# Preparing group A's first job inside the projection's stage

## The chip, the cores and the metric

The kernel runs on one core of a Trainium2 chip, in one launch. The metric is the device time of a run in microseconds, smaller is better. A core has five engines with a queue of instructions each, which they work off strictly in the order in which the program was laid out: TensorE (PE; its weight loads are listed as PEld), VectorE (DVE), ScalarE (ACT), GpSimd (POOL) and SyncE (SP, which here issues most of the transfers between HBM and SBUF). They wait for each other only through semaphores.

## The reference, cut to what matters

Two layers, 1024 tokens, width 1024. In each layer one input projection makes the columns of four head groups A to D, each group mixes the tokens in its own way, an output projection joins them, and a hierarchical mixture of experts follows. Everything is float32.

```python
h = rms_norm(x, norm1_g[l]) * (1 + sc1) + sh1
p = h @ w_in[l]                                  # 1024 x 3244
pA, pB, pC, pD = split_cols(p, (A_COLS, B_COLS, C_COLS, D_COLS))
yA = rwkv7_time_mix(pA, ...)       # A: state recurrence over the tokens
yB = stick_breaking_attn(...)      # B
yC = mlstm_mix(pC, ...)            # C: short convolution, then mLSTM
yD = dsa_attn(...)                 # D: top-256 keys per query, then attention
x = x + gt1 * (jnp.concatenate([yA, yB, yC, yD], -1) @ w_out[l])
x = x + gt2 * hier_moe(rms_norm(x, norm2_g[l]) * (1 + sc2) + sh2, ...)
```

The part of group A that this case is about is elementwise work on r, k, v, the decay and the in-context rate, before the recurrence runs:

```python
p = token_shift(p, mu)
r, k, v, wd, ad, gd = split_cols(p, A_SIZES)
kk = (k * k_k).reshape(B, S, H, d)
kk = kk / jnp.maximum(jnp.sqrt(jnp.sum(kk * kk, -1, keepdims=True)), 1e-12)
k = k * (1 + (a - 1) * k_a)
bonus = jnp.sum(r_h * k_h * r_k.reshape(H, d), -1, keepdims=True) * v_h
```

## The kernel before

**Stages of a layer.** First the hidden state is made and split into a high and a low float32r part, together with the indexer's columns of group D. Then comes the projection's stage, then the mixing stage with all four groups and the output projection, then routing and the experts. The two layers have the same stages; in layer 0 the mixing stage also computes the adaLN rows of later use (transfers and products named `aw`).

**The projection's stage.** `proj_rest` (L1933) goes through a list of jobs, one block of columns of `w_in` each. For each block it fetches the weights two blocks ahead (`fetch`, tiles `wr`), splits them one block ahead into `wh` (ScalarE) and `wl` (VectorE for the later blocks, L1863), and then runs the products. A block of 128 transposed columns is done in two halves of 512 tokens (`proj_t`, L1867), 24 products each into one PSUM tile `pj`, of which there are three. Seven blocks of group A come near the end, in the order 6, 0, 2, 4, 1, 3, 5 (here A6, A0, ...): A6 holds the low-rank inputs, A0 and A1 are r, A2 and A3 are k, A4 and A5 are v. The last four blocks are group C's, here C0 to C3. `take` (L255) empties a half of an A block: ScalarE makes `u`, VectorE makes `p` (L265), and SyncE stores `p` to HBM. `take_t` does so for C, with three VectorE operations L679, one L682 and a sigmoid (`cs`).

Beside it runs `select`, the search for each query's top 256 keys: rounds of counting on VectorE (L1022) and ScalarE (`eq`), each followed by small steps (L1087, L1089, L1084), and a tail (L1104 to L1111).

**Group A's jobs.** The recurrence is cut into four jobs (two column tiles ct by two halves hf of the tokens). `prep` (L287) prepares one: six transfers bring back what `take` and `lowrank` stored (L296 to L301), then a chain goes through all engines: a square on ScalarE, a product `pn` with a 0/1 matrix on TensorE, VectorE L307, ScalarE's Ln and Exp, VectorE L311, a scan L315, L314, L319 to L322, exponentials on ScalarE, L338 and the GpSimd operations L313 and L339 that make `ar`, L341, L342, L345, L346, a second product from `bon`, and L350. Each job then has four units; a unit starts with four transposes (L148, from `ar`, `kn`, `ks`, `v`) and small products into `pj`. `Rwkv.run` (L503) prepares the first job, then keeps three units going and prepares the later jobs beside them.

**What sets the order.** `weave` (L196) asks generators for their next piece of work, by a virtual clock that advances with the TensorE work that each has issued, and a generator that yields `WAIT` is asked again later. That gives the program order. From it the framework's scheduler lays out each engine's queue, with the program order as priority, and a tile can only be written once a buffer of its pool is free: 23 buffers in `big`, 38 in `med`. The queues are fixed before the kernel runs. Before the change, the first job was emitted by the first steps of `rw.run()`, in the second `weave`:

```python
weave(k, [(proj(), 257)], [(select(), 100)])
weave(k, [(rw.run(), 260)], [(dsr(), 350), (rest(), 140)], [(mods(), 550)], [(outs(), 150)])
```

`dsr` is group D's attention; its blocks for eight tiles of queries start with products into `a`, a masked maximum on VectorE (L1128, `dz`), an exponential on ScalarE, and transposes of `dz`.

Of the kernel before, what the change touches and what calls it, by code (L numbers as in the profile page):

```python
# [30 lines left out]
A0, B0, C0, D0 = 0, 896, 1664, 2696  # L31
# [63 lines left out]
class K:  # L95


    def __init__(self, ctx, tc, nbig, nmed, consts_dram):
        self.tc, self.nc, self.n = tc, tc.nc, 0
        self.ctx = ctx  # L100
        self.bigp = ctx.enter_context(tc.tile_pool(name="big", bufs=nbig))
        self.medp = ctx.enter_context(tc.tile_pool(name="med", bufs=nmed))
        self.cp = ctx.enter_context(tc.tile_pool(name="cp", bufs=1))
        self.sp = ctx.enter_context(tc.tile_pool(name="sp", bufs=2))
        self.ps = ctx.enter_context(tc.tile_pool(name="ps", bufs=1, space=PSUM))
        self.cst = self.cp.tile([P, NCONST], F32, name="cst")
        self.nc.sync.dma_start(self.cst, consts_dram[:, 0:NCONST])
        t = self.med("lev", 384)
        self.nc.sync.dma_start(t, consts_dram[:, NCONST:NCONST + 384])
        self.lev = self.cp.tile([P, 384], BF16, name="levb")  # L110
        self.nc.vector.tensor_copy(self.lev, t)
        self.evn, self.pe = 0, 0.0
        self.mode, self.mode_load, self.mode_acts = None, None, []
# [79 lines left out]
WAIT = -1.0  # L193


def weave(k, *streams):  # L196

    live = [[0.0, list(s)] for s in streams]
    while live:
        s = min(live, key=lambda x: x[0])
        gen, pace, *prio = s[1][0]
        before = k.pe
        try:
            if prio and prio[0]:
                with k.tc.high_priority(offset=prio[0]):
                    other = next(gen)  # L210
            else:
                other = next(gen)
        except StopIteration:
            s[1].pop(0)
            if not s[1]:
                live.remove(s)
            continue
        if other == WAIT and len(live) > 1:
            s[0] = 0.002 + min(x[0] for x in live if x is not s)
        else:  # L220
            s[0] += (k.pe - before + (other or 0.2)) / pace
# [23 lines left out]
class Rwkv:  # L245


    def __init__(self, k, pc, lw, rst, tk, l):
        self.k, self.pc, self.lw, self.rst = k, pc, lw, rst
        self.tk, self.l = tk, l  # L250
        self.s, self.y, self.done = {}, {}, set()

# [246 lines left out]
        yield  # L501

    def run(self, width=3):  # L503
        self.job = {}
        jobs = [(ct, hf) for hf in range(2) for ct in range(2)]
        yield from self.prep(*jobs[0])
        units = [(ct, 0, nb) for ct in range(2) for nb in range(4)] + [(ct, 1, nb) for nb in range(4) for ct in range(2)]
        ahead = {(0, 0, 1): jobs[1], (1, 0, 0): jobs[2], (1, 0, 2): jobs[3]}
        live, side = [], []
        k = self.k  # L510
        free = [(k.med("ra"), k.med("bkv", 384), k.med("mp"), k.med("tl")) for _ in range(width)]
        while units or live or side:
            while units and len(live) < width and units[0][:2] in self.job and "bon" in self.job[units[0][:2]]:
                u = units.pop(0)
                own = free.pop(0)
                live.append((u, self.unit(*u, own), own))
                if u in ahead:
                    side.append(self.prep(*ahead[u]))
            for it in list(live):
                try:  # L520
                    next(it[1])
                    yield
                except StopIteration:
                    live.remove(it)
                    free.append(it[2])
                    if it[0][2] % 2:
                        side.append(self.out(*it[0][:2], it[0][2] // 2))
            for g in list(side):
                try:
                    next(g)  # L530
                    yield
                except StopIteration:
                    side.remove(g)
# [1093 lines left out]
class Trunk:  # L1627
# [337 lines left out]
    def layer(self, l):  # L1965
        k, nc, ins = self.k, self.nc, self.ins
        pc = self.pc(l)
        ml = Mlstm(k, pc, self.gb, self.idb, self.mneg4.rearrange("p h t -> p (h t)"), self, l)
# [4 lines left out]
        rw = Rwkv(k, pc, self.lw, self.rst, self, l)  # L1973
        rw.eps = self.eps[:, 1:2]

        def take_b(j, h, ps):
# [4 lines left out]
            for x, st in enumerate((hi, lo)):  # L1981
                self.store_t(l, "b", 4 * x + j, h, st.bitcast(F32))

        bind = lambda f, j: lambda h, ps: f(j, h, ps)
        by_t = lambda c0, f, js: [(c0 + 128 * j, 128, lambda w, j=j: self.proj_t(w, bind(f, j))) for j in js]
        by_k = lambda c0, col, f: [(c0, 256, lambda w: self.proj_k(l, w, col, f))]
        bq = by_t(B0, take_b, range(4))
        jobs = (bq[:1] + by_k(B0 + 512, 0, AF.Copy) + [(D0 - 8, 264, lambda w: self.proj_q(ds, ml, w))]
                + bq[1:2] + by_k(C0 + 512, 256, AF.Copy) + bq[2:3]
                + [(C0 + 768, 256, lambda w: gate_out(w))] + bq[3:]  # L1990
                + by_t(A0, rw.take, (6, 0, 2, 4, 1, 3, 5)) + by_t(C0, ml.take_t, range(4)))

        def gate_out(w):
            ml.tanh()
            yield from self.proj_k(l, w, 512, AF.Sigmoid)

        def select():
            yield from ds.scores()
            yield from ds.search()

        sb = Stick(k, pc)
        sb.eps = self.eps[:, 0:1]
        stage = set()
        until = lambda f: iter(lambda: None if f() else WAIT, None)

        def proj():
            yield from self.proj_rest(l, jobs)
            stage.add("proj")
# [6 lines left out]
        def rest():  # L2015
            yield from until(lambda: "proj" in stage)
            ys[6], ys[7] = (both(ds.y, c) for c in range(2))
            ml.load(self, l)
            yield from ml.run()
            ys[4], ys[5] = (both(ml.y, c) for c in range(2))  # L2020
            yield from sb.run(self, l)

        def dsr():
            yield from until(lambda: "proj" in stage)
            yield from ds.run()
# [46 lines left out]
        def mods():  # L2072
            yield from until(lambda: "proj" in stage)
            if l == 0:
                yield from self.ada(0, [1])
            gt1.append(self.mod(l, 2))
            if l == 0:
                yield from self.ada(0, [2])
                yield from self.ada(1, [0, 1, 2])

        weave(k, [(proj(), 257)], [(select(), 100)])
        weave(k, [(rw.run(), 260)], [(dsr(), 350), (rest(), 140)], [(mods(), 550)], [(outs(), 150)])
        drain([moe.route()])
        gt2 = self.mod(l, 5)
# [128 lines left out]
```

## Time and profile before

| | us |
|---|---|
| median of three runs | 3555.73 |
| lowest and highest of them | 3541.35, 3557.87 |
| the profiled execution, its own time | 3548.04 |
| its span on the core | 3546.3 |
| TensorE busy | 3119.6 (88%) |
| VectorE busy | 2668.3 (75%) |
| ScalarE busy | 1953.8 (55%) |

How to read it: the profile is of one execution. Busy shares are averages over stages with different limits, so the stage around the change is read by itself: from windows (busy time of each engine, granted TensorE clock as a share of 2.4 GHz) and from the timeline (start, length, engine, line, operation, and in brackets the idle time before and who ended it). Matmuls overlap, so their rate is the distance between starts. In layer 0 the projection's stage lies before 433 us and the mixing stage behind it, in layer 1 the border is near 2191 us.

### The profile page before, as it was taken

What the parts mean: (1) busy time and instruction counts of PE and PEld (TensorE: products, weight loads), DVE (VectorE), ACT (ScalarE), POOL (GpSimd) and SP (SyncE); (2) the same over time, 40 slices, a digit from 0 to 9 for tenths busy, and PEclk for the clock granted to TensorE, in tenths of its full rate; (3) what the DMA queues carried; (4) which work ended last, traced back from release to release, by engine and by line L of the source; (5) the groups of instructions that cost most, each with busy time, mean ns of one, the idle gap of its engine ahead of it and who ended that gap; (6) DMA issues with size and microseconds to landing.
All of it is one profiled execution on the core that took longest, in us unless ns stands there. A gap on an engine that the chain in (4) does not pass through costs nothing. (4 is left out here: it accounts for less than half of the span.)

```text
span 3546.3 us, 58612 instructions
## 1 busy us (share of the span) xinstructions
PE 3119.6 (88%) x20960; PEld 2412.4 (68%) x20960; DVE 2668.3 (75%) x5190; ACT 1953.8 (55%) x3452; POOL 817.9 (23%) x769
## 2 busy tenths in 40 slices
PE   5988889989878899999968898988987889999996
PEld 3876645576656677777758766766665667877775
DVE  3589853467666899999975898556666689999995
ACT  3469333234443667777753782533444366777774
POOL 3220110113221225432212201011321221332231
PEclk8999989899887899999989998989988789999998
DMA  5233365443525799999942333124352479999996
GB/s 200 72 96 99 103 221 202 164 148 102 152 91 185 267 375 385 376 386 381 388 131 63 99 99 102 32 69 148 102 149 93 179 271 365 386 382 381 381 387 209
DMA packets 373685, 746.67 MB, mean 211 GB/s; under 512 B 44234, under 2 KB 108512, under 8 KB 373392
## 3 DMA queue, kind: packets, MB, share of 16 engines
q1 hardware_dynamic: 346880, 671.84, 52.5%
q0 software_dynamic: 20256, 70.33, 7.6%
q8 instruction: 167, 2.74, 0.3%
q10 hardware_dynamic: 6256, 0.74, 0.1%
q14 instruction: 126, 1.03, 0.1%
HBM read 635.26 MB, written 107.53 MB: 209 GB/s over the span
## 5 line engine op out<-in xcount | busy, mean ns | idle before, releaser
L160 ACT ACTIVATE wh<-wr 128x1024 fp32r<-128x1024 f32 (+3 forms) x900 | 887.9, 1006 | 297.1 <-DMA wr<-in_moe_w_dram 118.8
L1530 DVE TENSOR_TENSOR wl<-wr,wh 128x1024 fp32r<-128x1024 f32 x792 | 941.9, 1225 | 58.1 <-ACT wh L160 45.9
L143 PE MATMUL pj<-wl,xh 128*128 128x512 f32 x1056 | 419.5, 404 | 14.1 <-DVE wl L1530 13.7
L143 PE MATMUL pj<-wh,xh 128*128 128x512 f32 x1056 | 421.3, 400 | 11.7 <-ACT xh L160 10.3
L143 PE MATMUL pj<-wh,xl 128*128 128x512 f32 x1056 | 420.0, 398 | 0.0
L143 PEld LDWEIGHTS pj<-wl,xh 128*128 128x128 f32 x1056 | 200.4, 190 | 82.1 <-DVE wl L1530 37.8
L143 PEld LDWEIGHTS pj<-wh,xh 128*128 128x128 f32 x1056 | 199.9, 190 | 56.7 <-ACT xh L160 12.9
L143 PEld LDWEIGHTS pj<-wh,xl 128*128 128x128 f32 x1056 | 201.0, 190 | 45.5 <-DVE xl L1542 0.8
L143 PE MATMUL b<-wh,hh 128*128 128x512 f32 x528 | 210.9, 400 | 11.0 <-ACT wh L160 10.0
L1426 POOL DMA_INDIRECT xg<-h2d,si x64 | 76.3, 1193 | 606.1 <-PE a L148 349.7
L143 PE MATMUL b<-wh,hl 128*128 128x512 f32 x528 | 208.6, 395 | 1.1 <-DVE hl L1542 1.1
L143 PE MATMUL pj<-hh,wh 128*128 128x512 f32 x480 | 195.4, 409 | 8.8 <-ACT wh L160 8.4
L143 PE MATMUL pj<-hh,wl 128*128 128x512 f32 x480 | 195.9, 409 | 2.2 <-DVE wl L1863 2.2
L143 PE MATMUL pj<-hl,wh 128*128 128x512 f32 x480 | 194.2, 405 | 0.0
L1497 POOL DMA_INDIRECT xs<-yo,si x32 | 162.5, 5078 | 135.7 <-DVE yo L1494 111.1
L143 PE MATMUL pj<-wh,hl 128*128 128x256 f32 (+2 forms) x640 | 188.0, 296 | 1.8 <-DVE hl L1840 1.7
L143 PE MATMUL pj<-wh,hh 128*128 128x256 f32 (+2 forms) x640 | 182.0, 296 | 5.2 <-ACT wh L160 2.4
L143 PE MATMUL pj<-wl,hh 128*128 128x256 f32 (+2 forms) x640 | 184.2, 290 | 1.1 <-POOL wl L1863 1.1
L143 PE MATMUL b<-wl,hh 128*128 128x512 f32 x528 | 175.6, 412 | 6.9 <-DVE wl L1530 6.8
L1497 POOL DMA_INDIRECT out_dram<-yo,si x32 | 141.7, 4429 | 132.9 <-DVE yo L1494 116.7
L160 ACT ACTIVATE ra<-b 128x128 f32<-128x128 f32 (+1 forms) x192 | 54.1, 293 | 160.0 <-PE b L143 158.4
L143 PEld LDWEIGHTS pj<-wh,hh 128*128 128x128 f32 x640 | 121.5, 195 | 9.2 <-ACT hh L160 3.5
(526 smaller groups left out, 7374.0 us busy)
## 6 DMA issues: line engine op xcount, KB each, us to landing
wr<-in_moe_w_dram SPq DMA_DIRECT2D x792, 512.0 KB
aw<-in_ada_w_dram SPq DMA_DIRECT2D x96, 512.0 KB
wr<-in_w_in_dram SPq DMA_DIRECT2D x84, 256.0 KB
wo<-in_w_out_dram SPq DMA_DIRECT2D x48, 256.0 KB
xs<-xp SPq DMA_DIRECT2D x48, 256.0 KB
xp<-xs SPq DMA_DIRECT2D x48, 256.0 KB
out_dram<-xp SPq DMA_DIRECT2D x48, 256.0 KB
sk<-pt SPq DMA_DIRECT2D x32, 256.0 KB
```

Source lines behind the costliest of these rows:

```text
L143: return self.nc.tensor.matmul(out, lhsT, rhs, start=start, stop=stop, skip_group_check=True)
L160: i = self.nc.scalar.activation(out, in_, f, **kw)
L1426: i = self.k.nc.gpsimd.indirect_dma_start(out=xg, out_offset=None, in_=self.h2d, in_offset=bass.IndirectOffsetOnAxis(ap=gi.bitcast(U32), a ...
L1497: k.nc.gpsimd.indirect_dma_start(out=self.xs, out_offset=bass.IndirectOffsetOnAxis(ap=si.bitcast(U32), axis=0), in_=yo, in_offset=None, co ...
L1530: i = nc.vector.tensor_tensor(wl, raw, wh.bitcast(F32), op=ALU.subtract)
```

## The change

Group A's first job, ct 0 and hf 0, is now prepared by a third generator of the first `weave`, `first_job`. It waits until the second half of block A4 has been taken; with A6, A0 and A2 done before, all rows of that job exist then. `Rwkv.run` skips the preparation if it is there. Nothing is computed differently and no line inside `prep` changes.

```diff
-        self.s, self.y, self.done = {}, {}, set()
+        self.s, self.y, self.done, self.job = {}, {}, set(), {}
...
     def run(self, width=3):
-        self.job = {}
         jobs = [(ct, hf) for hf in range(2) for ct in range(2)]
-        yield from self.prep(*jobs[0])
+        if jobs[0] not in self.job:
+            yield from self.prep(*jobs[0])
...
+        def take_a(j, h, ps):
+            rw.take(j, h, ps)
+            stage.add(("a", j, h))
+
+        def first_job():
+            yield from until(lambda: ("a", 4, 1) in stage)
+            yield from rw.prep(0, 0)
...
-                + by_t(A0, rw.take, (6, 0, 2, 4, 1, 3, 5)) + by_t(C0, ml.take_t, range(4)))
+                + by_t(A0, take_a, (6, 0, 2, 4, 1, 3, 5)) + by_t(C0, ml.take_t, range(4)))
...
-        weave(k, [(proj(), 257)], [(select(), 100)])
+        weave(k, [(proj(), 257)], [(select(), 100)], [(first_job(), 100)])
```

**VectorE behind block A4, layer 0.** `p_3427` is the second half of A4; `wr_3347` and `wr_3349` are the raw weights of A3, and the `wl` made of them are its low parts. Before:

```order
L265 SCALAR_TENSOR_TENSOR p_3427<-pj_3401,drv,u_3426 128x512
L1087 TENSOR_TENSOR dth_2212<-dth_2212 128x3
L1089 SCALAR_TENSOR_TENSOR dth_2212<-dth_2212 128x3
L1084 TENSOR_SCALAR dth_2212<-dth_2212 128x3
L1863 TENSOR_TENSOR wl_3449<-wr_3347,wh_3448 128x512
L1022 TENSOR_SCALAR dkey_2215,dth_2212<-dkey_2215,dth_2212 128x768
```

Now the same split stands 45 rows behind `p_3427`; these are the last of them, with the job's own rows L322, L345, L350 and L346 and the search's between:

```order
L345 SCALAR_TENSOR_TENSOR bon_3488<-la_3433,prm,ks_3452 128x512
L1022 TENSOR_SCALAR dkey_2215,dth_2212<-dkey_2214,dth_2212 128x640
L1089 SCALAR_TENSOR_TENSOR dth_2212<-dth_2212 128x3
L322 TENSOR_TENSOR f_3465<-f_3465 128x7
L1022 TENSOR_SCALAR dkey_2216,dth_2212<-dkey_2214,dth_2212 128x384
L1084 TENSOR_SCALAR dth_2212<-dth_2212 128x3
L1087 TENSOR_TENSOR dth_2212<-dth_2212 128x3
L1022 TENSOR_SCALAR dkey_2215,dth_2212<-dkey_2215,dth_2212 128x768
L1089 SCALAR_TENSOR_TENSOR dth_2212<-dth_2212 128x3
L1863 TENSOR_TENSOR wl_3503<-wr_3347,wh_3502 128x512
L350 TENSOR_TENSOR bon_3488<-b_3491,v_3435 128x512
```

What moved: between `p_3427` and A3's first split lie now twelve counts L1022 of the search, with their small steps, and nine rows of the job (L307, L311, L315, L314, L319, L320, L321, L345, L322). On ScalarE, `wh_3502` stands in the same way behind the job's exponential of `cs`. In layer 1 it is ten counts and the same nine rows.

**TensorE at the end of the projection, layer 0.** The first row is the last product of block C3; `sq`, `bon`, `ar`, `kn`, `ks`, `v` are the job's tiles, `dz` and `dat` group D's. Before:

```order
L143 MATMUL pj_4106<-hl_348,wh_3957 128x512
L143 MATMUL pj_4238<-aw_4239,cz 32x512 x2
L143 MATMUL pj_4238<-aw_4241,cz 32x512 x2
L148 MATMUL pj_4257<-cst,dz_4226 128x128
L148 MATMUL pj_4261<-cst,dz_4247 128x128
L143 MATMUL b_4211<-sq_4209,cst 128x512
L143 MATMUL b_4264<-dat_4256,dv_325 64x128
L143 MATMUL b_4264<-dat_4260,dv_325 64x128
L143 MATMUL b_4304<-bon_4301,cst 128x512
L143 MATMUL a_4377<-dkh_439,dq_4222 128x384
```

Now:

```order
L143 MATMUL pj_4161<-hl_348,wh_4012 128x512
L148 MATMUL pj_4266<-cst,ar_3476 128x128
L148 MATMUL pj_4266<-cst,kn_3451 128x128
L148 MATMUL pj_4266<-cst,ks_3452 128x128
L148 MATMUL pj_4266<-cst,v_3435 128x128
L143 MATMUL pj_4273<-ar_3476,kn_3451 64x128 x2
L143 MATMUL pj_4273<-ar_3476,ks_3452 64x128 x2
L143 MATMUL pj_4279<-ar_3476,kn_3451 64x128 x2
L143 MATMUL pj_4279<-ar_3476,ks_3452 64x128 x2
L143 MATMUL pj_4302<-aw_4303,cz 32x512 x2
L143 MATMUL pj_4302<-aw_4305,cz 32x512 x2
L148 MATMUL pj_4321<-cst,dz_4289 128x128
```

What moved: the job's two products with the 0/1 matrix are gone from here (the first now stands inside the second half of A1, the second between A1 and A3), and the first unit's transposes and products stand right behind the projection, ahead of group D's transposes.

## Rows read from the trace of the kernel before

**Rows 1.** Windows: busy us (and count) by engine, granted clock, DMA share, GB/s.
```profile
330.00:400.00 70.00, 70.00 (x302) 56.73 (x301) 67.75 (x181) 40.66 (x78) 6.64 (x13) 1.00 0.30 93
433.00:458.00 25.00, 12.50 (x37) 4.04 (x35) 15.79 (x35) 9.43 (x24) 4.21 (x7) 0.59 0.55 186
443.90:450.50 6.60, 0.74 (x5) 0.35 (x5) 5.17 (x10) 2.77 (x6) 0.52 (x1) 0.50 0.98 362
460.00:1100.00 640.00, 566.23 (x5632) 381.94 (x5631) 370.50 (x858) 241.85 (x602) 118.05 (x189) 0.89 0.46 154
2191.00:2214.00 23.00, 9.08 (x23) 4.04 (x22) 14.90 (x33) 9.43 (x24) 4.04 (x6) 0.57 0.27 91
```

**Rows 2.** Timeline of TensorE, layer 0, from the projection's last product into the mixing stage.
```profile
433.00 0.40 PE L143 MATMUL pj<-hl,wh 128*128 128x512 f32 x1
...
440.68 0.86 PE L148 MATMUL pj<-cst,dz 128*128 128x128 f32 x2 [6.29 <-ACT dz L160]
...
450.35 2.07 PE L143 MATMUL b<-bon,cst 128*128 128x512 f32 x2 [5.86 <-DVE bon L345]
...
455.96 1.09 PE L148 MATMUL pj<-cst,dz 128*128 128x128 f32 x4
...
463.63 0.33 PE L148 MATMUL pj<-cst,ar 128*128 128x128 f32 x1
...
469.85 0.33 PE L148 MATMUL pj<-cst,ar 128*128 128x128 f32 x1
```

**Rows 3.** The same of layer 1.
```profile
2190.96 0.40 PE L143 MATMUL pj<-hl,wh 128*128 128x512 f32 x1
...
2212.56 1.18 PE L148 MATMUL pj<-cst,dz 128*128 128x128 f32 x4 [0.60 <-ACT dz L160]
...
2221.43 0.35 PE L148 MATMUL pj<-cst,ar 128*128 128x128 f32 x1
...
2225.33 0.27 PE L148 MATMUL pj<-cst,ar 128*128 128x128 f32 x1
```

**Rows 4.** Timeline of ScalarE, end of the projection: table load and two exponentials' groups.
```profile
438.84 1.28 ACT L154 ACT_TABLE_LOAD   x1
...
454.12 0.51 ACT L160 ACTIVATE dz<-dz,dnb 128x256 f32<-128x256 f32 x1 [3.29 <-DVE dnb L1132]
```

**Rows 5.** Timeline of VectorE: A4's second half in both layers, two search rounds.
```profile
351.94 0.75 DVE L265 SCALAR_TENSOR_TENSOR p<-pj,drv,u 128x512 f32<-128x512 f32 x1
...
359.75 0.88 DVE L1022 TENSOR_SCALAR_CACHE_REDUCE dkey<-dkey,dth 128x640 bf16<-128x640 uint16 x1
...
363.22 0.88 DVE L1022 TENSOR_SCALAR_CACHE_REDUCE dkey<-dkey,dth 128x640 bf16<-128x640 uint16 x1
...
2110.16 0.75 DVE L265 SCALAR_TENSOR_TENSOR p<-pj,drv,u 128x512 f32<-128x512 f32 x1
```

**Rows 6.** Timeline of ScalarE: A3's second half, taken as TensorE ends it, both layers.
```profile
371.98 0.69 ACT L160 ACTIVATE u<-pj,prm 128x512 f32<-128x512 f32 x1 [3.35 <-PE pj L143]
...
2130.11 0.69 ACT L160 ACTIVATE u<-pj,prm 128x512 f32<-128x512 f32 x1 [3.25 <-PE pj L143]
```

**Rows 7.** Timeline of TensorE behind its pause before block A0, layer 0.
```profile
323.09 0.79 PE L143 MATMUL pj<-hh,wh 128*128 128x512 f32 x1 [3.03 <-ACT wh L160]
...
325.25 0.63 PE L143 MATMUL pj<-hl,wh 128*128 128x512 f32 x1
...
330.37 0.50 PE L143 MATMUL pj<-hl,wh 128*128 128x512 f32 x1
330.71 0.39 PE L143 MATMUL pj<-hh,wh 128*128 128x512 f32 x1
```

**Rows 8.** Timeline of TensorE between blocks C1 and C2, layer 0.
```profile
404.90 0.40 PE L143 MATMUL pj<-hl,wh 128*128 128x512 f32 x1
...
408.30 0.49 PE L143 MATMUL pj<-hh,wh 128*128 128x512 f32 x1 [0.85 <-ACT wh L160]
...
409.70 0.63 PE L143 MATMUL pj<-hl,wh 128*128 128x512 f32 x1
```

More of the change, by code (lines that the diff above doesn't have):

```diff
@@ L1984, in layer @@
         bind = lambda f, j: lambda h, ps: f(j, h, ps)
+        stage = set()
+        until = lambda f: iter(lambda: None if f() else WAIT, None)
+        def take_a(j, h, ps):
[4 more added lines that the diff above has]
+            yield from rw.prep(0, 0)
         by_t = lambda c0, f, js: [(c0 + 128 * j, 128, lambda w, j=j: self.proj_t(w, bind(f, j))) for j in js]
@@ L2002, in layer @@
         sb.eps = self.eps[:, 0:1]
-        stage = set()
-        until = lambda f: iter(lambda: None if f() else WAIT, None)
         def proj():
```

## The prediction

> **What bounds the kernel now.** I read the windows first, then the timeline on both sides of the border between the projection and the mixing stage. In the projection's last part TensorE is the limit with VectorE right beside it: from 330 to 400 us TensorE is busy 70.0 of 70 us at the full clock (302 products, so one every 0.232 us, and a half block of 24 takes 5.56 us), and VectorE 67.8 of 70 [rows 1]. At the border TensorE starves: of the 25 us from 433 it is busy 12.5 at a granted clock of 0.59, of the 23 us from 2191 only 9.1 at 0.57 [rows 1]. The reader is to see two waits in it: 6.3 us for group D's first exponential, and 5.9 us for the job's `bon` on VectorE [rows 2]. After that TensorE is busy 566 of 640 us [rows 1], so the mixing stage is near its limit, but not at it.
>
> **The change, part by part.**
>
> *What leaves the border.* The first job's chain goes. In layer 0 the projection's last product starts at 433.00, so TensorE is free at E = 433.2; group D's second pair of transposes starts at 455.96, the transposes of the second and third unit at 463.63 and 469.85 [rows 2]. In layer 1: E = 2191.2, then 2212.56, 2221.43 and 2225.33 [rows 3].
>
> What is late next is group D's exponential. It comes behind group C's last sigmoid and a table load of 1.28 us [rows 4], and its transposes start 440.68 - 433.2 = 7.5 us after E [rows 2]. None of that moves, and two evacuations of the first unit now go ahead of it (0.6 us, an estimate by the exponential of 128 x 256 in [rows 4], which is of like size): 8.1. The next pair follows one masked maximum and two exponentials of 0.51 us later [rows 4], an estimate of 2 us: its transposes start at E + 10.1 instead of E + 22.8. From there the queue has the same pieces as before with a unit one further on, so before's way from 455.96 to 463.63, 7.7 us [rows 2], leads to the third unit: E + 17.8. In layer 1 that way is 8.9 us [rows 3], so E + 19.0.
>
> *What enters the projection: VectorE.* E does not stay where it is. The job is emitted right behind A4, before A3's weights are split, so it stands ahead of them in the order, and the title's "beside group C" is not where most of it lies. A3's `wl` now comes behind twelve counts of the search and nine rows of the job. Twelve counts are four double rounds of 363.22 - 359.75 = 3.47 us [rows 5], 13.7 without the last small step. The nine rows: VectorE was busy 5.17 us between 443.9 and 450.5, in ten instructions, one of them a copy of group D (0.3, estimated from what the nine leave): 4.9 [rows 1]. A4's `p` starts at 351.94 and takes 0.7 [rows 5], so A3's first low part is there at 352.6 + 13.7 + 4.9 + 0.6 = 371.8. When does TensorE want it? The second half of A3 ended at 371.9 before [rows 6], so A3 began 48 x 0.232 = 11.1 us earlier, at 360.8; one product of the job now lies ahead, 2.07 us at the low clock [rows 2], so 1.0 at the full one: 361.8. Wait: 10.0 us. The second product of the job lies within it.
>
> Layer 1: ten counts (11.7 us), so 2110.16 + 0.7 + 11.7 + 4.9 + 0.6 = 2128.1 [rows 5]; A3 would be wanted at 2130.1 - 11.1 + 1.0 = 2120.0 [rows 6]. Wait: 8.1 us.
>
> *The clock behind that wait.* After pauses of such a kind in layer 0 the products came every (330.37 - 325.25) / 12 = 0.427 us, the 1.2 GHz level, from 323.09 until 330.71 [rows 7], about 17 of them: 17 x 0.195 = 3.3 us. I take this for each layer. Bounds: nothing, if the clock holds, and twice as much.
>
> *The later waits.* Between C1 and C2 TensorE paused from 405.1 to 408.3 and came back at the low level (0.63 us a product) [rows 8]: 3.2 us and some 2 for the clock. C2's weights are split behind the search's tail and C0's evacuation. The job's six other rows and its nine put that tail some 9 us later, TensorE is about 10 later, so this pause shrinks: I give back 4 us. Bounds: 5 back, or 5 more.
>
> So E moves by 10.0 + 1.0 + 3.3 - 4 = 10.3 us in layer 0 and 8.1 + 1.0 + 3.3 - 4 = 8.4 in layer 1.
>
> *The other queues.* ScalarE gets the job's seven operations and one table load more per layer; it was busy 40.7 of 70 us [rows 1], and A3's `wh` comes before its `wl`, so VectorE ends the wait. On SyncE the job's first four transfers stand ahead of A3's raw weights, but these are asked for nearly two blocks ahead, over 20 us, so that hides them; without that cover A3 would wait for them instead. GpSimd's part ends long before a unit needs it. Nine `med` buffers are held through the projection: the order already contains that, as A1's evacuations now stand behind A3's split.
>
> *Sum.* Layer 0: group D's second pair at 433.2 + 10.3 + 10.1 = 453.6 instead of 455.96, 2.4 us sooner; the third unit at 461.3 instead of 469.85, 8.5 sooner. Layer 1: 2209.7 for 2212.56, 2.9 sooner; 2218.6 for 2225.33, 6.7 sooner. If the rest is bound by group A's chain of units, the gain is 15.2 us, if by the other streams and TensorE's work, 5.3. With 88% busy neither has it alone, so I take 10 us. The rest of the program has the same work, in an order that differs by a few dozen rows here and there.
>
> The profiled execution took 3548.0, so 3538; the median of the three runs is 7.7 higher, so 3546. I start from halfway, 3552, and say 3542 us.
>
> **Rivals.**
>
> *The whole gain (3523).* A3's weights are not late, since A1 to A5 have slack that I do not see. Then E stays and 18.7 us come on top: 24 to 34 us, in the middle 29. For it: TensorE loses its pause at the border. Against it: VectorE has 2.2 us free in 70 [rows 1] and gets 10 more per layer. The Trainium skill ("Perfetto Trace Analysis", Optimization Strategy) says that regimes with different most-contended engines may gain by being interleaved. By that rule this rival is the outcome. The trace agrees only by half, as the stage that takes the job in has its VectorE full too.
>
> *Nothing (3552).* The mixing stage is bound by TensorE's sum of work and idle time. The border loses 12.5 us of idle time and part of a low clock, and gets 10 and 8 us of idle time and a low clock in the projection in return. For it: 88% busy [rows 1]. Against it: units wait for each other in a chain, and that chain starts earlier.
>
> *Slower (3567).* The wait spreads: with VectorE full, each later split (A5, C0, C2) also comes some 4 us late, so that E moves by 10 + 12 = 22. The start of the mixing stage is then late for both streams. It decides from where the gain is used up: for group D at 455.96 - 10.1 - 433.2 = 12.7 us in layer 0 and 11.3 in layer 1, for the units at 18.9 and 15.1. At 22 and 20 that is 3 to 9 us per stream and layer, 13 to 15 in sum, and beyond 25 it is over 20. For it: the tail of the search (L1104 to L1111) is VectorE's densest part. Against it: once the search is over VectorE has room. The Trainium skill ("Perfetto Trace Analysis", Optimization Strategy) has a rule that speaks this way too: bubbles that repeat on the engine which should be saturated can mean that buffers ran out for the next tile. No row of before shows it, as TensorE is busy throughout 330 to 400.
>
> **How the numbers follow.** The forecast gets 0.5, the whole gain 0.15, nothing 0.2, slower 0.15. The forecast's own range is 3530 to 3555. 0.5%, about what a measurement of this kernel can tell from no change, is 17.8 us. Faster by more: the whole gain and a fifth of the forecast, 0.25. Slower by more: two thirds of the slower case, and a little of the two middle ones, for a reordered schedule: 0.12. The rest, 0.63, is within. The range runs from 3518, below the whole gain, to 3570, which leaves out the upper end of the slower case.
>
> **What would show it.** Right: a pause of TensorE of 8 to 10 us between A1 and A3, ended by VectorE's `wl` (L1863), with 0.43 us products behind it; the projection's end 8 to 10 us later, relative to its start; at the border no wait for `bon`, the first unit's transposes at once, then a wait of some 6 us for `dz`; the third unit's transposes 18 to 19 us after E. Wrong: no pause before A3 (the whole gain), further pauses before A5, C0 or C2 (slower), or the third unit earlier by 7 to 8 us and the mixing stage's end not (nothing).

## The result

The changed kernel is slower: a median of 3570.48 us (3562.19 to 3585.65, seven runs) beside 3550.55 us of the kernel before on the same chip (3539.83 to 3557.87, seven runs), a ratio of 1.0062 with a 95% interval of 1.0046 to 1.0078. I forecast 3542 us.

Where the time went is read from five stretches of the two profiled executions. Their borders are group D's second masked maximum (VectorE, `dz` of 128 x 256), with which its queue is under way, and the first row of routing (`sm`, L1272), which ends the mixing stage.

| stretch | before | after | difference |
|---|---|---|---|
| start to group D's second maximum, layer 0 | 452.06 | 448.19 | -3.9 |
| from there to routing, layer 0 | 705.68 | 720.56 | +14.9 |
| from there to group D's second maximum, layer 1 | 1052.10 | 1052.52 | +0.4 |
| from there to routing, layer 1 | 631.93 | 649.51 | +17.6 |
| from there to the end | 704.5 | 700.5 | -4.0 |

The stretches that hold the projection, the job and the border, the whole subject of the prediction, changed by -3.9 and +0.4 us. The loss lies in the mixing stage behind them, which has the same work as before. The last stretch, layer 1's routing and experts, which the edit leaves alone, differs by 4.0 us too, so a few us between two single executions say little. (Line numbers from L1985 on are 8 to 11 higher in the changed kernel.) These are the mixing stage's two windows, TensorE alone, in the kernel before (stretch, its length, busy time and count of products, granted clock, DMA share, GB/s):

```profile
452.06:1157.74 705.68, 616.82 (x5872) 0.88 0.46 155
2209.84:2841.77 631.93, 542.71 (x5560) 0.86 0.35 111
```

and in the changed kernel:

```profile
448.19:1168.75 720.56, 626.28 (x5856) 0.88 0.46 156
2221.27:2870.78 649.51, 560.30 (x5544) 0.83 0.34 109
```

The same products, up to 16 that now lie outside the window, keep TensorE busy 9.5 and 17.6 us longer; its idle time is 88.9 and then 94.3 us in layer 0, 89.2 both times in layer 1. In layer 1 the granted clock falls from 0.86 to 0.83; 0.03 of 649.5 us is 19 us (an estimate), so there the loss is not waiting but products that run at the low clock. In layer 0 the granted clock is 0.88 both times, so 5.4 us are idle time, and the clock over the whole stage does not explain the other 9.5; what does stays open.

Two further runs below, gp and aft_sp2, have nearly the order of the changed kernel. In them it took 724.8 and 723.4 us in layer 0, but 637.0 and 634.4 in layer 1. So layer 0's loss comes back, while of layer 1's 17.6 us only 5.1 and 2.5 do: that size is one execution's. TensorE's busy time grows over the whole program too, as the page's first part shows:

```profile
span 3571.3 us, 58590 instructions
...
PE 3145.1 (88%) x20960; PEld 2419.7 (68%) x20960; DVE 2671.6 (75%) x5190; ACT 1963.0 (55%) x3456; POOL 802.2 (22%) x769
```

Before, TensorE was busy 3119.6 us: 25.5 us less, and the span is 25.0 us longer.

**The projection of the changed kernel.** The rows that answer to [rows 1], for 330 to 400 and 433 to 458 us:

```profile
330.00:400.00 70.00, 64.82 (x261) 50.52 (x260) 67.89 (x187) 44.92 (x85) 4.82 (x16) 0.93 0.33 103
433.00:458.00 25.00, 20.43 (x113) 12.68 (x111) 13.09 (x31) 10.02 (x27) 3.65 (x8) 0.86 0.54 196
```

TensorE has lost 5.2 of 70 us ahead of A3, at a lower clock, and won 7.9 of 25 us at the border. Its timeline shows the pause and who ended it, first in layer 0 (two rows), then in layer 1:

```profile
365.12 2.08 PE L143 MATMUL b<-bon,cst 128*128 128x512 f32 x2 [4.33 <-DVE bon L345]
...
368.48 0.80 PE L143 MATMUL pj<-hh,wl 128*128 128x512 f32 x1 [0.85 <-DVE wl L1863]
...
2140.47 2.08 PE L143 MATMUL b<-bon,cst 128*128 128x512 f32 x2 [7.55 <-DVE bon L345]
```

The wait is for `bon`, since the job's second product stands ahead of A3's in TensorE's queue, and `wl` adds 0.85 us only. The border, where [rows 2] had the products of `dz` at 440.68 and 455.96 and the third unit's transposes at 469.85:

```profile
439.70 0.39 PE L143 MATMUL pj<-hl,wh 128*128 128x512 f32 x1
439.94 0.27 PE L148 MATMUL pj<-cst,ar 128*128 128x128 f32 x1
...
447.47 0.86 PE L148 MATMUL pj<-cst,dz 128*128 128x128 f32 x2 [1.59 <-ACT dz L160]
...
450.76 1.05 PE L148 MATMUL pj<-cst,dz 128*128 128x128 f32 x4
...
460.98 0.33 PE L148 MATMUL pj<-cst,ar 128*128 128x128 f32 x1
```

The projection ends 6.7 us later, the first unit starts in the same microsecond, group D's second pair is 5.2 us and the third unit 8.9 us ahead of before. The same in layer 1:

```profile
2212.82 0.39 PE L143 MATMUL pj<-hl,wh 128*128 128x512 f32 x1
2213.05 0.27 PE L148 MATMUL pj<-cst,ar 128*128 128x128 f32 x1
...
2223.84 1.05 PE L148 MATMUL pj<-cst,dz 128*128 128x128 f32 x4
...
2230.19 0.27 PE L148 MATMUL pj<-cst,ar 128*128 128x128 f32 x1
```

**One place in the reordered mixing stage.** In layer 0 most of the 14.9 us lie in group C's part, between group D's last tile and group C's last: 145.8 us before, 159.3 after. There the output projection's `x` comes late. SyncE's queue, then VectorE and TensorE in the changed kernel:

```profile
717.90 0.33 SPq L2154 DMA_DIRECT2D xs<-xp  x1
719.92 0.33 SPq L2152 DMA_DIRECT2D xp<-in_x_dram  x1
720.30 0.43 SPq L1962 DMA_DIRECT2D ld<-pk  x1
720.78 0.50 SPq L2152 DMA_DIRECT2D xp<-in_x_dram  x1
...
723.80 0.69 DVE L2134 TENSOR_TENSOR xp<-pj,xp 128x512 f32<-128x512 f32 x1 [3.40 <-DMA xp<-in_x_dram]
...
724.55 0.50 PE L143 MATMUL pj<-woh,yh 128*128 128x512 f32 x1 [3.26 <-DVE xp L2134]
```

The load of `x` stands behind the store of the tile before it, which waited for VectorE. TensorE stands still for 3.3 us, and then the windows of TensorE read:

```profile
716.00:720.00 4.00, 4.00 (x74) 1.00 0.18 66
720.00:724.00 4.00, 1.29 (x23) 1.00 0.70 208
724.00:728.00 4.00, 3.45 (x20) 0.69 0.34 124
728.00:732.00 4.00, 4.00 (x23) 0.50 0.00 0
732.00:736.00 4.00, 4.00 (x12) 0.50 0.40 131
736.00:740.00 4.00, 4.00 (x16) 0.61 0.00 0
```

From 724 to 740 it is busy nearly throughout, mostly at the 1.2 GHz level; in the kernel before the granted clock is 1.00 from 700 to 760 us. The wait of 3.3 us costs about twice as much again behind it (an estimate: 16 us at a mean clock of 0.58 hold 9.2 us of work at the full one, so 6.8 us are lost). The Trainium skill ("TensorE: Matmul & The Clock Gate", HAM oscillation) describes this: a wait for a transfer between bursts of products lowers the clock, and the products behind it pay. The trace agrees, with the rows above.

### The profile page after: what moved, and what is told of

It is laid out like the page before. It is cut to its first block, busy times and chain, and to the rows that moved or that the text cites. A ratio compares the mean times of both kernels' runs of the same rounds, so it can differ in the third digit from the quotient of the medians.

```text
span 3571.3 us, 58590 instructions
## 1 busy us (share of the span) xinstructions
PE 3145.1 (88%) x20960; PEld 2419.7 (68%) x20960; DVE 2671.6 (75%) x5190; ACT 1963.0 (55%) x3456; POOL 802.2 (22%) x769
## 5 line engine op out<-in xcount | busy, mean ns | idle before, releaser
L1497 POOL DMA_INDIRECT xs<-yo,si x32 | 135.9, 4247 | 134.9 <-DVE yo L1494 110.1
L143 PE MATMUL pj<-woh,yh 128*128 128x512 f32 x256 | 121.0, 475 | 14.2 <-DVE xp L2134 4.9
```

What stands on the lines that cost most here:

```text
L143: return self.nc.tensor.matmul(out, lhsT, rhs, start=start, stop=stop, skip_group_check=True)
L1497: k.nc.gpsimd.indirect_dma_start(out=self.xs, out_offset=bass.IndirectOffsetOnAxis(ap=si.bitcast(U32), axis=0), in_=yo, in_offset=None, co ...
```

## The experiments

Two theories stood against each other from the start. **Delay:** the projection ends later by what the job costs there, this comes out at the end whole, and the early start is worth nothing. **Order:** the starts are as good as before or better, and the loss comes from the order in which the mixing stage is now laid out. The order changes because `Rwkv.run` no longer spends the virtual time of four pieces, so its units come a little ahead of the other generators. Counted on the traces (successive rows of TensorE with the same operation, names and shapes taken as one, and the longest sequence in common), 10,860 of 11,960 rows stand in the same sequence before and after.

All ratios are to the kernel before, run on the same chip, with 95% intervals.

**Runs both, none, tr_c1, tr_c3.** both prepares the job in the projection and once more in the mixing stage, and so keeps the order of before:

```diff
-        if jobs[0] not in self.job:
-            yield from self.prep(*jobs[0])
+        yield from self.prep(*jobs[0])
```

> The first job is prepared twice: in the projection's stage as in the changed kernel, and once more at the border, whose result the units use; the border and the mixing stage keep the order of before. Delay theory (what the projection loses, 10 us a layer, comes out at the end whole, and the job's early start is worth nothing): before + 20 us, as the changed kernel. Order theory (the projection's delay is hidden by slack of the mixing stage, and the loss comes from the mixing stage's new order): before + 0 to 5 us.

Measured: 1.0054 (1.0033 to 1.0076), 17.8 us by the medians. That is the job's cost in the projection, and it does come out at the end. From group D's second maximum on the mixing stage took 705.8 and 633.0 us, as before (705.7 and 631.9). Here the delay theory was right.

none leaves the preparation out:

```diff
+        if (ct, hf) == (0, 0):
+            ...
+            for x in t5[:5] + [ar, f]:
+                G.memset(x, 0.0)
+            ...
+            return
```

> The kernel before, with the first job's preparation left out (its tiles are zeroed by GpSimd, so the results of group A are not the reference's): the most that freeing the border of it can give, at no cost to the projection. My prediction's step (the mixing stage gains 15 us by its streams and units starting earlier): before - 15 to - 30 us. Delay theory, where the early start is worth nothing: before - 5 to 0. Order theory: it may be slower than before, + 5 to + 15, as its mixing stage is reordered too.

Measured: 1.022 (1.0193 to 1.0246), slower by 78 us, with less work. A part of it can't be read: from layer 0's routing to group D's second maximum in layer 1 it takes 49.6 us more, and with other values the experts can get other tokens (TensorE has 21,109 products for 20,960). Layer 0's mixing stage can be read: group D's second maximum is at 437.1, 14.9 us sooner than before, and routing at 1164.0, 6.3 us later. An early start for nothing was lost again. No theory of mine had more than + 15.

tr_c1 and tr_c3 let the job in later, behind blocks C1 and C3:

```diff
         def first_job():
-            yield from until(lambda: ("a", 4, 1) in stage)
+            yield from until(lambda: ("c", 1, 1) in stage)
```

> The changed kernel with the job let in later, behind block C1, where the search on VectorE is over but for its tail; A3's split stands where it stood before. Delay theory: the loss goes, before - 5 to + 5 us. Order theory: the mixing stage has nearly the order of the changed kernel, so the time stays at before + 15 to + 20. My prediction's step on the early start: before - 10 to - 20, as the gain is there without the wait.

> The changed kernel with the job let in behind the last block of the projection, so that it stands at the border again, and only the order of the mixing stage is that of the changed kernel. Delay theory: before - 3 to + 3 us. Order theory: before + 15 to + 20.

Measured: 1.0154 (1.0135 to 1.0173) and 1.0129 (1.0107 to 1.0151). Both numbers are far above all expectations, and a new wait is part of it, so they don't decide between the theories. VectorE in tr_c1:

```profile
423.41 0.74 DVE L345 SCALAR_TENSOR_TENSOR bon<-la,prm,ks 128x512 f32<-128x512 f32 x1
425.92 2.28 DVE L1108 TENSOR_TENSOR_SCAN pre<-eq 128x1024 f32<-128x1024 bf16 x1
429.74 0.68 DVE L341 TENSOR_TENSOR kn<-kn,lb 128x512 f32<-128x512 f32 x1
430.34 1.48 DVE L1108 TENSOR_TENSOR_SCAN pre<-eq 128x640 f32<-128x640 bf16 x1
...
455.47 0.28 DVE L1128 CUSTOM_DVE_ANT_0 dz<-a,zd 128x128 f32<-128x128 f32 x1
```

Before, the first of these scans of the search's tail started at 376.71 us and the first `dz` at 408.97. Now the first scan comes behind the job's last read of `la` and the second behind that of `lb`. `pre`, `la` and `lb` are tiles of the one pool `big`, so I read it as the tail waiting for the job's buffers; that wasn't tried by itself. Behind `dz` the mixing stage of layer 0 was 729.5 and 722.4 us long.

**Runs pad, ordctl, gp, pad_gp.** pad changes only the order: `Rwkv.run` yields what the preparation would have taken.

```diff
         if jobs[0] not in self.job:
             yield from self.prep(*jobs[0])
+        else:
+            yield from (1.0533, 0.2, 0.2, 1.0533)
```

> The changed kernel, in which group A's generator lets as much of the weave's virtual time pass as the preparation took there before, so that the mixing stage is laid out in nearly the order of before; the job stays in the projection. Order theory (group D starts 4 us sooner in layer 0 and as before in layer 1, and the new order makes the mixing stage 15 and 18 us longer): the loss goes, before - 6 to + 4 us. Delay theory (the projection's delay is passed on whole and nothing is gained): before + 15 to + 20, as the changed kernel.

Measured: 0.9992 (0.9975 to 1.0009). TensorE's sequence has 11,658 rows in common with the kernel before. The loss is gone, with the job still in the projection; the wait for `bon` is still there (4.8 us). Against the changed kernel's 1.0062 it is 0.7% less: some 25 us were the order's. Its windows of the mixing stage:

```profile
450.01:1160.00 709.99, 615.11 (x5876) 0.88 0.47 159
2212.85:2841.90 629.05, 543.11 (x5564) 0.86 0.36 112
```

With both this gives the border's worth: the same projection, nearly the same order, and without the second preparation 0.62% less, 22 us (some 12 to 32, by the two intervals). It is used up by the 18 us that the projection pays.

ordctl is the counterpart: the kernel before, with the order of the changed one (11,766 rows in common with it, 10,851 with before).

```diff
-        yield from self.prep(*jobs[0])
+        k, g = self.k, self.prep(*jobs[0])
+        while jobs[0] not in self.job or "bon" not in self.job[jobs[0]]:
+            p0 = k.pe
+            next(g)
+            yield p0 - k.pe + 1e-6
```

> The kernel before, its projection and its border unchanged, in which the preparation of the first job takes no virtual time, so that the mixing stage is laid out in nearly the order of the changed kernel. Order theory: before + 20 to + 35 us. Delay theory: before - 3 to + 3.

Measured: 1.0104 (1.008 to 1.0128), 38.7 us by the medians, 23.7 in the profiled execution. The order theory holds in its size only with a part that I hadn't reckoned: the job's rows now stand ahead of group D's at the border, whose second maximum comes 6.3 us later in layer 0 and 7.5 in layer 1. The mixing stage behind it is 2.5 and 9.9 us longer, 12.4 of the 23.7, where the changed kernel had 32.5.

gp has A3's low parts made by GpSimd, pad_gp has that and the order of before.

```diff
-        eng = lambda i: self.nc.gpsimd if i < 9 else self.nc.vector
+        eng = lambda i: self.nc.gpsimd if i < 9 or i == 13 else self.nc.vector
```

> The changed kernel with A3's low parts made by GpSimd, so that they don't stand behind the job on VectorE; the mixing stage keeps the order of the changed kernel. TensorE's wait before A3 should go, and group D starts 8 to 10 us sooner in each layer. Order theory and delay theory both say before + 0 to + 6 us, as the starts come out at the end and the order still costs its share; if the wait before A3 is no cost of the changed kernel, it stays at + 20.

> Both edits: the order of before in the mixing stage and A3's low parts on GpSimd. Order theory: before - 25 to - 12 us, faster than both kernels, since the border's gain is left without the wait and without the new order. Delay theory: before - 5 to + 3, as the early start is worth nothing.

Measured: gp 1.0067 (1.0045 to 1.0089), pad_gp 0.9978 (0.996 to 0.9996). `wl` was not what TensorE waited for: in gp it waits 5.6 us for `bon`, and then 0.35 us for GpSimd's `wl`. pad_gp is the only run whose interval lies below the kernel before, by 3.5 us of the medians and 8 by the ratio. The wait is no shorter in it, 5.3 us for `bon`, so what its few us come from isn't shown.

**Runs dep1, best1, pace255, pace265.** dep1 is pad with the job's second product ordered behind A3's last, and best1 adds the low parts on GpSimd.

```diff
+        last = k.last
         pb = k.psum("b")
-        k.mm(pb, k.c("blk64"), bon)
+        i = k.mm(pb, k.c("blk64"), bon)
+        if gate:
+            k.order(getattr(i, "ins", i), getattr(last, "ins", last))
```

> The run pad (order of before in the mixing stage) with one more edit: the job's second product is tied behind A3's last product, so that TensorE no longer waits for bon ahead of A3 (4.8 us there, with some 8 us at the low clock behind it). If that wait and the low clock are what the projection lost: 5 to 8 us less per layer, before - 16 to - 8 us. If A3 then waits for its wl instead, as my prediction has it: as pad, before - 5 to + 3.

> The run dep1 with A3's low parts on GpSimd too, so that neither bon nor VectorE's wl stands ahead of A3's products: no pause of over 2 us between A1 and A3; before - 25 to - 10 us, the fastest of all. If the projection's end then still moves by 4 us or more, something else in it (A3's wh, the pause between C1 and C2) takes the wait's place: before - 8 to 0.

Measured: 1.0012 (0.9996 to 1.0028) and 1.0000 (0.9984 to 1.0015). For dep1 I had named `wl` as the next wait; in it TensorE waits longer than in pad, and for ScalarE, whose `wh` of A3 stands behind the job's exponentials and the search's counts. best1, whose second branch named `wh`, has the same wait of 6.3 us. The rows of dep1:

```profile
368.84 0.80 PE L143 MATMUL pj<-hh,wh 128*128 128x512 f32 x1 [6.26 <-ACT wh L161]
370.76 0.79 PE L143 MATMUL pj<-hh,wl 128*128 128x512 f32 x1 [1.12 <-DVE wl L1871]
```

The two others ask what an order is worth at all. Nothing of the change is in them; one number of the kernel before is another:

```diff
-        weave(k, [(rw.run(), 260)], ...
+        weave(k, [(rw.run(), 265)], ...
```

> The kernel before with nothing moved but the pace of group A's generator in the second weave, 255 for 260: the same work, the same projection, and a mixing stage as much reordered against before as the changed kernel's. If the order of before is simply a good one and any other of this size costs: before + 10 to + 40 us. If only an order with group A's units ahead costs: before - 5 to + 5, as A is a little slower here. If small changes of the order don't matter: within 3 us.

> As pace255, with 265 for 260, so that group A's units get a little ahead, as they do in the changed kernel. Any other order costs: before + 10 to + 40 us. Only an order with group A ahead costs: before + 10 to + 30. Small changes of the order don't matter: within 3 us.

Measured: 1.0168 (1.0146 to 1.0191) and 1.0209 (1.0185 to 1.0232), 62 and 72 us. That is three times the loss of the changed kernel, in either direction of the pace, so it takes no lead of group A to lose. The mixing stage of pace265:

```profile
449.07:1180.80 731.73, 630.97 (x5872) 0.87 0.44 150
2233.94:2909.80 675.86, 567.27 (x5560) 0.83 0.32 103
```

Its counts of products are those of before, and it is 26.1 and 43.9 us longer: 11.9 and 19.4 of that TensorE is idle, the rest it is busy longer, at a granted clock of 0.87 and 0.83 (before: 0.88 and 0.86).

**Runs sp2, sp2dep, aft_sp2, pace262.** The first three split A3's weights a block sooner, ahead of the job: sp2 on pad, sp2dep on dep1, aft_sp2 on the changed kernel.

```diff
-            if i + 1 < len(jobs):
-                w.append(self.split(raws[i + 1], jobs[i + 1][1], eng(i + 1)))
+            while len(w) < min(len(jobs), i + (3 if i == 11 else 2)):
+                w.append(self.split(raws[len(w)], jobs[len(w)][1], eng(len(w))))
```

> The run pad (order of before in the mixing stage) with A3's weights split one block sooner, so that A3's high and low parts stand ahead of the job on ScalarE and VectorE. If the wait before A3 (bon, then wh, then wl) is what the projection lost and its end counts: before - 16 to - 8 us. If the wait only moves on to A5's split, which now stands behind the job, or the end does not count: before - 4 to + 4.

> As sp2, with the job's second product tied behind A3's last one, so that neither bon, wh nor wl can hold A3: no pause of over 2 us between A1 and A3. If the projection's end counts: before - 20 to - 10 us. If not: before - 4 to + 4.

> The changed kernel, its mixing stage in its own order, with A3's weights split one block sooner. If half of the loss is the wait before A3: before + 5 to + 12 us. If the loss is the order's alone: before + 17 to + 25, as the changed kernel.

Measured: 1.0025 (1.0014 to 1.0036), 1.0025 (1.0011 to 1.0038) and 1.0042 (1.0026 to 1.0059). sp2 and sp2dep are some 9 us slower than the kernel before, outside what I had expected of either. In sp2 the pause ahead of A3 is down to 2.3 us, ended by A1's evacuation `p`. TensorE's waits between 340 and 436 us (for whom, us in total, times, the longest) and two of its windows:

```profile
PE a L143 <- DMA dq<-pt: 3.0, 2, 1.9
PE pj L143 <- DVE p L265: 2.3, 1, 2.3
PE a L143 <- DVE dmx L1130: 2.2, 1, 2.2
```

```profile
360.00:370.00 10.00, 7.70 (x28) 0.92 0.12 33
410.00:420.00 10.00, 6.12 (x18) 0.66 0.54 192
```

Now group D's first products, among block C's, wait for `dq` and `dmx`, and from 410 to 420 us TensorE is busy 6.1 us at a clock of 0.66, where before it was busy all of the 10 us at 0.87. So the wait went from `bon` to `wh`, to `p` and `dmx`, and was never taken away. In the order of the changed kernel the earlier split may be worth 0.2%; the intervals of 1.0042 and 1.0062 overlap. And aft_sp2 and sp2 differ by the order alone, as the changed kernel and pad do, but by 0.17% with overlapping intervals, and not by 0.7%. In sp2's profiled execution the mixing stage of layer 0 took 720.2 us, as long as the changed kernel's, though 11,680 of its rows keep the order of before; layer 1 took 622.8. So keeping that much of the order is no guard by itself.

> The kernel before with group A's pace at 262 for 260, a smaller shift than 255 and 265: it still moves some 1500 of TensorE's rows. If the time falls off with the distance from the order of before: before + 10 to + 40 us, less than pace255 and pace265. If any reordering costs about the same: before + 40 to + 75. If those two are oddities: within 10 us.

Measured: 1.0076 (1.0059 to 1.0093), 24 us: less than 255 and 265, with a smaller move of the order (11,204 rows in common with before; 10,927 and 10,994 for those two). Three paces don't make a rule for distance, but all three are slower.

## Why the prediction was wrong

**The projection: right in its sum, wrong in the wait.** I had its end 10.3 and 8.4 us later, 18.7 in all; the trace shows 6.7 and 10.8 (the latter less the 11.0 us by which layer 0 ended later), 17.5 in all, and the run both has 17.8 us more in its time. By layer it fits less well: ahead of the job's first product TensorE stood 0.8 us sooner than before in layer 0 (a product at 348.42, before 349.25) and 2.1 later in layer 1 (2120.57, before 2107.48, less the 11.0), so the job cost 7.5 and 8.7. In layer 0 the wait was the term too large, 10.0 us: I had A3's `wl` there at 371.8, and it ended at 368.4, since A4's `p` started 1.9 us sooner than before and the rows between took 17.7 us for 19.2. The 4 us given back between C1 and C2 came out (3.4 and 3.1), though the 3.2 us that I read there as a pause hold four products of group D and 2.1 us of idle time. And the wait is ended by `bon`, not by `wl`. I had put the job's second product within the wait and not asked what it waits for itself: it stands ahead of A3 in TensorE's queue, and VectorE makes `bon` as one of the job's last rows. Behind it `wh` would have been late too, which I had excluded.

**The border: right in its direction, and near in part by luck.** Group D's second transposes start at 450.8 us (453.6 forecast, 455.96 before), the third unit at 461.0 (461.3 forecast, 469.85 before). But TensorE was free at 439.9, not at 443.5, and the third unit came 21.1 us behind that, not 17.8: two misses that cancel. In layer 1, less 11.0 us: 2212.8 (2209.7 forecast, 2212.56 before) and 2219.2 (2218.6 forecast, 2225.33 before), so the second pair gained nothing there.

**The step that failed** is the sentence "The rest of the program has the same work, in an order that differs by a few dozen rows here and there", costed at nothing; of the chances a reordered schedule had only a little of the 0.12 for slower. In the profiled executions it cost 14.9 and 17.6 us of the mixing stage. That it is the order, and not the job's place, is shown by pad, where the order of before put back ends the loss (0.9992), and by the paces of 255, 262 and 265, which make one with no change at all (0.8 to 2.1%). ordctl (1.0104) points the same way, but more than half of the loss in its profiled execution lies ahead of the mixing stage. How much an order costs seems to hang on the kernel around it: the three pairs that differ by it alone are 0.70% (the changed kernel and pad), 0.89% (gp and pad_gp) and 0.17% (aft_sp2 and sp2, not clear of noise) apart.

**What the starts are worth.** With the order kept, the border's gain is 22 us (both to pad, 12 to 32); I had 24 to 34 for all of it. It meets 18 us in the projection, and pad is 0.5 us faster than before by the medians (the interval: 9 us faster to 3 slower). My 10 us were too much there as well, and "nothing" was the rival that fits it.

**The slower rival** had 3567 us, close to the time, by a mechanism that isn't there: no further waits before A5, C0 or C2 made the border late. Its number came out by chance.

**What stays open:** which rows of the new order cost, one by one. The late load of `x` is one: a wait of 2.1 to 3.7 us for `xp` in group C's part of layer 0 shows in after, gp, tr_c1, tr_c3, ordctl and none, and one of at most 0.7 in before, both, pad and pad_gp. Layer 1 of the changed kernel has none there, but one of 4.1 us for `xp` at 2614 us, where the kernel before has none over 0.4 in its layer 1. Neither was taken away by itself, and pace265, which loses three times as much, has no wait for `xp` over 1.7 us in either layer, so it can't be the whole.

## What to carry to other kernels

Where a scheduler lays out the queues from a program order, an edit has two parts: the work that it moves, and the order that it gives to everything behind. Measure the second by itself, with a version that makes the edit and keeps the old order, and with the old kernel under another order of the same kind; without them a gain of some 22 us and a loss of 18 would have been buried under some 25 us that have nothing to do with either. And a wait that is ended by one queue often has the next late one right behind it: look at what would end it next before pricing its removal.

## What the runs showed of the hardware

A profile's idle times don't show what a low clock costs. Between before and after TensorE's idle time in the mixing stage grew by 5.4 us in layer 0 and by nothing in layer 1; its busy time for the same products grew by 9.5 and 17.6 us. In layer 1 the granted clock fell with it, from 0.86 to 0.83, and with pace265 the same way; in layer 0 it was 0.88 both times. I had priced the clock only behind the projection's waits, as 3.3 us a layer.
